# Second block of a transformer kernel: window attention's projections by token tiles, two ScalarE steps in the recurrence's operands

## The chip, the cores and the metric

The program runs on one core of a Trainium2 chip as one launch. The metric is the device time of that core in microseconds (us). Three runs of the kernel before took 4450.48, 4458.26 and 4474.45 us; their median is 4458.26 us.

## The reference

A two-part network over 1024 tokens of 1024 features: a first block (two mixers, each followed by a mixture of experts, in float32), and a second block, which the change touches. Of the second block only its start matters here. It normalises the tokens x and 256 context tokens, multiplies both with one projection `w_in`, and cuts the columns of the result into queries, keys and values of a window attention, the inputs of a recurrence, and gates:

```python
h  = modulate(rmsnorm_2(x, norm1_g), shift1, scale1)
hc = modulate(rmsnorm_2(xc, norm1_g), modc[0], modc[1])
q, k, v, rw, gl = jnp.split(h @ w_in, IN_SPLITS, axis=-1)       # 512, 128, 128, 1696, 2048 columns
qc, kc, vc, rwc, glc = jnp.split(hc @ w_in, IN_SPLITS, axis=-1)
q = apply_rope(q.reshape(B, L, N_Q_HEADS, HEAD_DIM), cos, sin)
k = apply_rope(k.reshape(B, L, N_KV_HEADS, HEAD_DIM), cos, sin)
ya = latent_window_attention(q, k, v, kc, vc, sink)
r_l, v_l, hg_l, kk_l, dirs_l = rwkv_prepare(short_conv(rw, conv_w), decay_w0, decay_w2,
                                            iclr_a0, iclr_a2, k_k, k_a)
# in rwkv_prepare, for two directions d, with k the recurrence's keys:
#   w_log = -softplus(-(decay_w0[d] + tanh(hw) @ decay_w2[d])) - 0.5
#   a = sigmoid(iclr_a0[d] + ha @ iclr_a2[d]);  k_d = k * (1 + (a - 1) * k_a)
```

## The kernel before

Every float32 operand of a product is split into two float32r parts, a high one (`hi`, a ScalarE copy, L111) and the rest (`lo`, a VectorE subtraction, L116), and a product is three matmuls (high by high, low by high, high by low). The eight PSUM banks are shared out by use: here A 3, S 2, T 2 (transposes) and M 1.

The start of the second block is `block2` (L1163). Its stages follow each other in this order.

1. Norms, `block2_norms` (L1229): eight token tiles of 128 x 1024 in pairs. For a pair, squares on ScalarE (L1261) and a weighted sum of them on VectorE (L1262) give the factors; VectorE scales (`ht`, L1272), GpSimd adds the shift (L1273). `to_hT` transposes a tile on TensorE (L185, eight transposes of 128 x 128 into two banks of T) and splits it into `hH` and `hL`, features by tokens. Two context tiles go the same way into `cH` and `cL`.
2. Low ranks and gate of the recurrence, in `Rwkv.project` (L1531): `conv(W, 0, 64, 12, ..)` and `conv(W, 64, 96, 13, ..)` (L1582, L1583). A `conv` is a product of up to 128 features with all tokens, in token pieces of 512, 512 and 256, that is 24 matmuls of each, and a convolution of three taps. Their weights, 160 columns, are loaded before the norms' tokens.
3. The operand stage: four times (`ft`) two `conv` of 128 features (keys `uk`, receptances `ur`), `norms` (L1670, whose first matmuls are L1684), and `operands` (L1697), which goes through three token pieces and two directions. There a tanh on ScalarE (L1717) is followed by `l + 1` on VectorE (L1718), prefix sums (L1721), exponentials and products on VectorE, and on GpSimd `kd = ta * kh0 + kh1` (L1741) with two products (L1742, L1743). A matmul into bank M (L1754) takes `kd` at the end of a piece.
4. Four `conv` of the recurrence's values, and what is left of the window.

The window's projection is the generator `Window.project` (L1369). Its first piece makes keys and values of ten token tiles: 24 matmuls of 128 x 256, a ScalarE copy `qo` (L1398), the rotation of the keys on VectorE (`rotate`, L832 to L837), transposes, `qkH`, `qkL`, and stores to `wv_d` and `wk_d`. The second and third pieces make the two halves of the queries (L1407), eight tiles of 128 x 256 each. `more` hands them out: the first behind `operands` of ft 0, the second behind ft 1, the third at the end (L1591, L1200). The instructions of the engines are put in order by a scheduler that follows this program order by dependencies and buffers, so that window work is spread over the stage that follows.

Of the kernel before, what the change touches and what calls it, by code (L numbers as in the profile page):

```python
# [34 lines left out]
D = 1024  # L35
# [8 lines left out]
class K:  # L44
    """Engines, pools and the few operations that every phase uses."""
# [62 lines left out]
    # float32 as the sum of two float32r parts, exact  # L108
# [9 lines left out]
    def row_max(s, pool, todo, mx):  # L118
        """Largest of scores + mask by rows, one column of mx each."""
# [5 lines left out]
    def to_rows(s, pool, cols, n, *dst):  # L125
        """The negatives of columns, one after the other in rows of partition 64."""
# [13 lines left out]
    def weights(s, raw, ring, src, shape, leng=None, queue=None):  # L140
        """A block of weights, loaded and split."""
# [11 lines left out]
    def rstd(s, ss, n, scale, eps, name):  # L153
        """(ss * scale + eps) ** -0.5, few elements per partition."""
# [6 lines left out]
    def bcast(s, pool, ap, n, name, parts=128, **kw):  # L161
        """A row of n values in DRAM on every partition."""
# [5 lines left out]
    def norm_pair(s, pool, xs, gb, outs, eps=EPS, gb2=None):  # L168
        """Two token tiles normalised over their 1024 features and scaled by gb (plus gb2)."""
# [11 lines left out]
    def transpose4(s, src, n=4):  # L181
        """Four [128, 128] blocks of a token tile, transposed into one PSUM bank."""
# [5 lines left out]
    def to_hT(s, src, hH, hL, t):  # L188
        """A token tile [128, 1024] into features by tokens, split."""
# [12 lines left out]
# ---------------------------------------------------------------- even mixer  # L202
# [4 lines left out]
def even_mixer(k, es_out, x_d, w, mod_d):  # L207
    """x_d: DRAM [1024, 1024]. w: DRAM inputs. Returns the output projection and what it takes. The second
    block's modulation goes by the way."""
# [42 lines left out]
def proj_tile(k, hH, hL, W, t, n):  # L252
    """h of token tile t times a block of weights given in chunks of two k-tiles."""
# [74 lines left out]
def even_project(k, es, w, raw, ring, hH, hL, q_d, k_d, v_d):  # L328
    """Queries, keys and values, rotated, in their two parts: q_d, k_d [part, head, feature, token], v_d [part, head,
    token, feature]."""  # L330
# [36 lines left out]
NQ = 4  # heads whose operands are on chip at a time  # L367
# [31 lines left out]
def even_head(k, p2, mb, mc, me, h, slot, q_d, k_d, v_d, a_d, r_d):  # L399
# [13 lines left out]
    # values, by tokens shifted by half a tile and by residue classes of 4  # L413
# [12 lines left out]
    with k.tc.high_priority(offset=HP):  # L426
        # row maxima of both key sets
# [28 lines left out]
    def attend():  # L456
# [21 lines left out]
        # band of 64 tokens to either side  # L478
# [3 lines left out]
        def pv(b, c, v, P):  # L482
            # one accumulation group per bank: what is not yet written is overwritten
# [25 lines left out]
        # dilations 4 and 16, within the residue classes of 4  # L509
# [16 lines left out]
def normalise(k, p2, O, r_row, dst, shape=None, more=None):  # L526
    """Rows 0..63 of O over its row 64 into DRAM. more adds to the row, spread over the partitions."""
# [12 lines left out]
class OutProj:  # L540
    """x + a @ w_out by token tiles; a: features by tokens in DRAM, one tile of 128 features each."""
# [40 lines left out]
# ---------------------------------------------------------------- mixture of experts  # L582
# [5 lines left out]
class Moe:  # L588
    """Expert choice over the tokens of x1; x_d gathers x1 and what the experts add to it."""

    def __init__(s, k, es, i, w, x_d):
# [8 lines left out]
        # the router takes the tokens before their norm: its weights by the norm's  # L600
# [38 lines left out]
    def rank(s, x, last):  # L639
        """The best of every expert so far and these: in order, but for the last time."""  # L640
# [9 lines left out]
        if s.best is not None:  # L650
            # the best of two lists: the one against the other from its end; then sorted
# [14 lines left out]
    def choose(s):  # L666
        """Which slot of which expert a token takes: those above the last of the best by their order, then the
        first of its equals."""
        k, p = s.k, s.p1
        # token number and gate in parts that bfloat16 carries exactly  # L670
# [19 lines left out]
        # how many up to a token, and how many above in all  # L690
# [16 lines left out]
    def gather(s, p, e):  # L707
        """The tokens of an expert, their numbers and gates."""
# [18 lines left out]
    def experts(s):  # L727
        k, w, i = s.k, s.w, s.i
        s.es.close()
        with ExitStack() as es:  # L730
# [11 lines left out]
            # in the order of use: the first products of an expert go ahead of the last of the expert before  # L742
# [65 lines left out]
# ---------------------------------------------------------------- odd mixer  # L808
# [31 lines left out]
def odd_mixer(k, es_out, x_d, w):  # L840
    """x_d: DRAM [1024, 1024]. w: DRAM inputs. Returns the output projection and what it takes."""
    a_d = [k.dram.tile([128, T], F32, name=f"a_do{i}") for i in range(8)]
    r_d = k.dram.tile([16, T], F32, name="r_d1")
    # operands of the attentions in their two parts, features by tokens, by heads or pairs of heads
# [25 lines left out]
def odd_proj(k, es, x_d, w, d):  # L870
# [23 lines left out]
    # ranks: queries, keys and values, rotary keys  # L894
# [27 lines left out]
    def heads(x, n, g, r, t):  # L922
        """Norms and rotations of n heads of a token tile."""
# [8 lines left out]
    def split_rows(src, dst, half, m):  # L932
        """Four token tiles' columns src(t) as features by tokens, split, into dst[part]."""
# [50 lines left out]
    # from the ranks to the heads  # L984
# [39 lines left out]
def odd_attention(k, es, d, a_d, r_d):  # L1024
# [13 lines left out]
    def head(n, h):  # L1038
# [25 lines left out]
        # row maxima of the scores, negated, into a row of the queries' operand  # L1064
# [41 lines left out]
# ---------------------------------------------------------------- second block  # L1106

TC = 256  # context tokens
C = 64  # tokens of a chunk of the recurrence
# [53 lines left out]
def block2(k, x_d, w, mod_d, out):  # L1163
# [7 lines left out]
    with ExitStack() as es:  # L1171
# [28 lines left out]
        for _ in more:  # L1200
            pass
# [1267 lines left out]
```

## Time and profile before

| | |
|---|---|
| runs, median | 4458.26 us (4450.48 to 4474.45) |
| the profiled execution, span | 4467.4 us |
| TensorE busy, mean granted clock | 3963.4 us (89%), 0.928 of full speed |
| VectorE, ScalarE, GpSimd busy | 66%, 41%, 25% |
| the stages of the change | 2248 to 2722 us of the span |

The trace gives one execution, and every time in the sections below is counted from the start of its span. A granted clock of 1.00 is TensorE's level of 2.4 GHz, one of 0.50 its level of 1.2 GHz; values between them are a mixture over the stretch. In a timeline a matmul's duration is its time from first to last of a pipeline, so the distance of two starts tells the cost of one.

### The profile page before, as it was taken

To read this page: it belongs to the slowest core of one execution; us is meant where nothing else is said; L and a number is where in the kernel's file an instruction comes from. 1 tells how busy PE (TensorE), PEld (TensorE's weight loads), DVE (VectorE), ACT (ScalarE), POOL (GpSimd) and SP (SyncE) were. 2 spreads that over 40 slices of the span, in tenths; PEclk is the share of its full clock that TensorE was granted. 3 is DMA by queue.
4 is the path that set the end of the run, shared out by engine and by line. 5 is a ranking of instruction groups with operands and counts; after the bars stand their busy time and mean duration, and the time that the engine had idled before them with its cause. 6 is when DMAs were issued, how large, how long until landed. Compare 5 with 4: busy or idle time off the path is not lost. (4 is left out here: it accounts for less than half of the span.)

```text
span 4467.4 us, 65652 instructions
## 1 busy us (share of the span) xinstructions
PE 3963.4 (89%) x24208; PEld 3233.3 (72%) x24208; DVE 2938.6 (66%) x5925; ACT 1815.5 (41%) x3066; POOL 1109.1 (25%) x1069
## 2 busy tenths in 40 slices
PE   7898995897978999689948997999988899999998
PEld 7797884775855666567737776777777678888887
DVE  8656658896678875879866793766677565332334
ACT  3223332675447775257634452333333432212212
POOL 2211212121213433112133363222244511101101
PEclk9998997999989999889968998989998999999999
DMA  5758435898267543569933446555756662111112
GB/s 163 228 170 187 110 112 186 304 367 279 82 189 176 116 102 93 188 238 365 329 111 118 148 148 181 138 142 137 166 145 147 190 210 88 57 48 48 49 55 85
DMA packets 568286, 714.12 MB, mean 160 GB/s; under 512 B 243636, under 2 KB 355332, under 8 KB 567964
## 3 DMA queue, kind: packets, MB, share of 16 engines
q1 hardware_dynamic: 467788, 510.50, 37.3%
q0 software_dynamic: 42480, 144.62, 11.9%
q10 hardware_dynamic: 57696, 54.80, 3.8%
q8 instruction: 191, 3.13, 0.3%
q14 instruction: 131, 1.07, 0.1%
HBM read 555.84 MB, written 153.53 MB: 159 GB/s over the span
## 5 line engine op out<-in xcount | busy, mean ns | idle before, releaser
L116 DVE TENSOR_TENSOR w_l<-w_raw,w_h 128x2048 fp32r<-128x2048 f32 (+5 forms) x336 | 592.2, 1769 | 194.1 <-ACT w_h L111 192.9
L111 ACT ACTIVATE w_h<-w_raw 128x2048 fp32r<-128x2048 f32 (+4 forms) x344 | 507.2, 1487 | 437.4 <-PE psO L138 254.5
L138 PE MATMUL psA<-w_h,hH 128*128 128x256 f32 (+3 forms) x896 | 292.6, 330 | 28.9 <-ACT w_h L111 13.7
L138 PE MATMUL psA<-w_l,hH 128*128 128x256 f32 (+3 forms) x896 | 292.6, 327 | 1.9 <-DVE w_l L116 1.7
L138 PE MATMUL psA<-w_h,hL 128*128 128x256 f32 (+3 forms) x896 | 291.3, 326 | 0.0
L116 POOL TENSOR_TENSOR uL<-relu,uH 128x512 fp32r<-128x512 f32 x64 | 82.6, 1291 | 571.9 <-ACT uH L111 571.9
L138 PE MATMUL psA<-w_h,xH 128*128 128x512 f32 x512 | 208.5, 409 | 11.6 <-ACT xH L111 8.8
L138 PE MATMUL psA<-w_l,xH 128*128 128x512 f32 x512 | 211.1, 412 | 7.1 <-DVE w_l L116 6.9
L138 PE MATMUL psA<-w_h,xL 128*128 128x512 f32 x512 | 206.1, 404 | 4.3 <-DVE xL L116 4.3
L138 PEld LDWEIGHTS psA<-w_h,hH 128*128 128x128 f32 x896 | 174.5, 196 | 41.6 <-ACT w_h L111 15.1
L2287 DVE TENSOR_TENSOR relu<-relu 128x512 f32<-128x512 f32 x64 | 44.3, 693 | 238.2 <-ACT relu L2286 238.2
L116 DVE TENSOR_TENSOR PL<-P,PH 128x512 fp32r<-128x512 f32 x192 | 171.1, 903 | 27.3 <-ACT PH L111 27.1
L138 PEld LDWEIGHTS psA<-w_l,hH 128*128 128x128 f32 x896 | 175.3, 196 | 10.4 <-DVE w_l L116 4.6
L138 PE MATMUL psA<-ghH,gwH 128*128 128x256 f32 x512 | 169.6, 331 | 14.5 <-DMA ghH<-hs_d 5.0
L138 PEld LDWEIGHTS psA<-w_h,hL 128*128 128x128 f32 x896 | 175.1, 195 | 5.3 <-issue 2.6
L805 POOL DMA_INDIRECT x_d<-yo,idx x32 | 69.8, 2182 | 421.5 <-ACT yo L804 417.5
L111 ACT ACTIVATE gwH<-gw 128x256 fp32r<-128x256 f32 x256 | 103.3, 414 | 163.1 <-PE psA L138 121.0
L138 PE MATMUL psA<-ghH,gwL 128*128 128x256 f32 x512 | 161.2, 315 | 1.3 <-POOL gwL L116 1.0
L138 PE MATMUL psA<-ghL,gwH 128*128 128x256 f32 x512 | 160.4, 313 | 0.0
L116 POOL TENSOR_TENSOR gwL<-gw,gwH 128x256 fp32r<-128x256 f32 x128 | 97.5, 765 | 248.3 <-ACT gwH L111 207.5
L111 ACT ACTIVATE PH<-P 128x512 fp32r<-128x512 f32 x256 | 154.5, 629 | 6.5 <-POOL PL L116 1.3
L116 POOL TENSOR_TENSOR PL<-P,PH 128x512 fp32r<-128x512 f32 x64 | 90.9, 1420 | 231.2 <-ACT PH L111 178.2
(654 smaller groups left out, 11896.8 us busy)
## 6 DMA issues: line engine op xcount, KB each, us to landing
w_raw<-in_moe_w_gate_dram SPq DMA_DIRECT2D x64, 1024.0 KB
w_raw<-in_moe_w_up_dram SPq DMA_DIRECT2D x64, 1024.0 KB
w_raw<-in_moe_w_down_dram SPq DMA_DIRECT2D x64, 1024.0 KB
gw<-in_w_in_t_dram POOLq DMA_DIRECT2D x64, 512.0 KB, 5.5
wada<-in_w_ada_dram POOLq DMA_DIRECT2D x48, 512.0 KB, 5.8
w_raw<-in_w_mlp_up_dram SPq DMA_DIRECT2D x16, 1024.0 KB
w_raw<-in_w_mlp_down_dram SPq DMA_DIRECT2D x16, 1024.0 KB
AR<-ar_d SPq DMA_DIRECT2D x40, 256.0 KB
```

Source lines behind the costliest of these rows:

```text
L111: s.a.activation(h, x, AF.Copy)
L116: (eng or s.v).tensor_tensor(l, x, f(h), op=ALU.subtract)
L138: s.t.matmul(ps, a, b, start=first and i == 0, stop=last and i == n - 1)
L805: k.g.indirect_dma_start(out=s.x_d[:, :], out_offset=off, in_=y, in_offset=None, compute_op=ALU.add)
L2287: k.v.tensor_tensor(a, a, a, op=ALU.mult)
```

## The change

The window's keys, values and first half of the queries are made inside the norms: right behind the transposes of token tile t, `done(t)` multiplies it by 512 columns of weights at once (keys, values, first half of the queries), copies, rotates, transposes, splits and stores. The four weight blocks of 128 x 2 x 512 (2 MB) and the tables `cosW`, `sinW` are loaded ahead of the norms' tokens. The pools of the later weights are opened behind the norms, in the same space. The second half of the queries (`A.rest`) comes behind `R.project`, as before. In `operands` the steps `l + 1` and `kd` go to ScalarE.

```diff
@@ block2
-        raw = k.pool(es, "b_raw", 2)
-        ring = k.pool(es, "b_ring", 5)
+        A.open_project(es)
+        with ExitStack() as es1:
+            block = blocks(k.pool(es1, "b_raw1", 4), k.pool(es1, "b_ring1", 4))
+            tile_ = A.first(block, hH, hL, cH, cL)
+            block2_norms(k, w, x_d, mod_d, hH, hL, cH, cL, rs, tile_)
+        block = blocks(k.pool(es, "b_raw", 2), k.pool(es, "b_ring", 5))
         p0 = k.pool(es, "rp0", 1)
-        block2_norms(k, w, x_d, mod_d, hH, hL, cH, cL, rs)
         R.ranks_weights(p0)
...
-        more = A.project(es, block, hH, hL, cH, cL)
-        R.project(block, hH, hL, cH, cL, more, stores())
-        for _ in more:
-            pass
+        R.project(block, hH, hL, cH, cL, stores())
+        A.rest(block, hH, hL)
@@ block2_norms
                 k.to_hT(h, hH, hL, t)
+                done(t)
-        ca = k.bcast(p1, mod_d[7], D, "ca")
-        cs = k.bcast(p1, mod_d[6], D, "cs")
+        ca = k.bcast(p1, mod_d[7], D, "ca", tag="g2")
+        cs = k.bcast(p1, mod_d[6], D, "cs", tag="gf")
...
             k.to_hT(xs[t], cH, cL, t)
+            done(8 + t)
@@ Window
+    def first(s, block, hH, hL, cH, cL):
+        k = s.k
+        W = block((512, 0))
+
+        def tile_(t):
+            ps = proj_tile(k, hH, hL, W, t, 512) if t < 8 else proj_tile(k, cH, cL, W, t - 8, 256)
+            o = s.pp.tile([128, 256], F32, name="qo")
+            k.a.activation(o, ps[:, 0:256], AF.Copy)
+            k.a.dma_start(s.v_d[128 * t:128 * t + 128], o[:, 128:256])
+            s.store(o[:, 0:128], 2, s.k_d, t, t < 8)
+            if t < 8:
+                o = s.pp.tile([128, 256], F32, name="qo")
+                k.a.activation(o, ps[:, 256:512], AF.Copy)
+                s.store(o, 4, s.q_d[:, 0:4], t, True)
+
+        return tile_
@@ Rwkv.project
-                for _ in range((1, 1, 0, 0)[ft]):
-                    next(more)
@@ Rwkv.operands
-                k.v.tensor_scalar(l, l, 1.0, None, op0=ALU.add)
+                k.a.activation(l, l, AF.Copy, bias=1.0)
...
-                k.g.tensor_scalar(kd, ta, s.kh[:, ft, 0:1], s.kh[:, ft, 1:2], op0=ALU.mult, op1=ALU.add)
+                k.a.activation(kd, ta, AF.Identity, scale=s.kh[:, ft, 0:1], bias=s.kh[:, ft, 1:2])
```

How this moves the instructions is seen in their order on two engines. First TensorE before, at the start of the norms: `psO` is the last product of the experts, `ht` a normalised token tile, `hH` and `hL` its transposed parts, and the products 64 wide are those of the low ranks.

```order
L138 MATMUL psO<-w_h,yL 128x512
L185 MATMUL psT<-c_ident,ht 128x128 x28
L138 MATMUL psA<-hH,w_h 64x512
L185 MATMUL psT<-c_ident,ht 128x128 x8
L138 MATMUL psA<-hL,w_h 64x512
L138 MATMUL psA<-hH,w_l 64x512
```

Three and a half tiles are transposed in one go, and the products between later ones are single products of the low ranks. TensorE after, from the last matmul of one token tile's product to the first of the next's (`qo` holds keys or queries; in brackets the semaphores that a row waits for):

```order
L138 MATMUL psA<-w_h,hL 128x512
L185 MATMUL psT<-c_ident,qo 128x128 [waits DVE_49,Activation_49]
L185 MATMUL psT<-c_ident,qo 128x128 [waits DVE_49,PE_49,Activation_49]
L185 MATMUL psT<-c_ident,qo 128x128
L185 MATMUL psT<-c_ident,ht 128x128 [waits DVE_49,Pool_49]
L185 MATMUL psT<-c_ident,ht 128x128 x3
L185 MATMUL psT<-c_ident,ht 128x128 [waits DVE_49]
L185 MATMUL psT<-c_ident,ht 128x128 x3
L138 MATMUL psA<-w_h,hH 128x512 [waits Activation_49]
```

The transposes of the next token tile now stand behind those of this tile's keys and queries, and all 24 matmuls of a tile stand together. The products of low ranks and gate follow the last context tile. VectorE before, in the norms' first tiles:

```order
L116 TENSOR_TENSOR w_l<-w_raw,w_h 128x512
L116 TENSOR_TENSOR hL<-psT,hH 128x4x128
L156 TENSOR_SCALAR m_n_20792<-ss_20778 128x2
L116 TENSOR_TENSOR hL<-psT,hH 128x4x128
L1264 COPY rs<-r_n_20840 128x2
L1266 TENSOR_TENSOR ss_20831<-ss_20831,r_n_20840 128x2
L1262 ISA sq,ss_20884<-sq,g_20703 128x1024
```

VectorE after, between the same two products (`rot_2` are the keys' products in the rotation, `rot_4` the queries'):

```order
L833 TENSOR_TENSOR rot_4_32_20845<-qo,sinW 128x128
L834 TENSOR_TENSOR rot_4_32_20846<-qo,sinW 128x128
L835 TENSOR_TENSOR rot_4_32_20847<-qo,cosW 128x128
L836 TENSOR_TENSOR qo<-rot_2_32_20824,rot_2_32_20825 128x2x32
L837 TENSOR_TENSOR qo<-rot_2_32_20826,rot_2_32_20827 128x2x32
L836 TENSOR_TENSOR qo<-rot_4_32_20844,rot_4_32_20845 128x4x32
L837 TENSOR_TENSOR qo<-rot_4_32_20846,rot_4_32_20847 128x4x32
L116 TENSOR_TENSOR qkL<-psT,qkH 128x128
L116 TENSOR_TENSOR qkL<-psT,qkH 128x256
L116 TENSOR_TENSOR hL<-psT,hH 128x4x128
```

The sums of both rotations stand behind the queries' products, and `hL` of the next tile behind both `qkL`; the statistics of all tiles (`ss`, `m_n`) have moved ahead of the first rotation. VectorE before, in the operand stage:

```order
L1738 TENSOR_TENSOR ar<-r,F 128x8x64
L1745 TENSOR_TENSOR bf<-ta,E 128x8x64
L1718 TENSOR_SCALAR l<-l 128x256
L116 TENSOR_TENSOR qkL<-psT,qkH 128x256
L832 TENSOR_TENSOR rot_4_32_22920<-qo,cosW 128x128
L833 TENSOR_TENSOR rot_4_32_22921<-qo,sinW 128x128
L834 TENSOR_TENSOR rot_4_32_22922<-qo,sinW 128x128
L835 TENSOR_TENSOR rot_4_32_22923<-qo,cosW 128x128
L116 TENSOR_TENSOR qkL<-psT,qkH 128x256
L1721 SCALAR_TENSOR_TENSOR F<-reset,l 128x256
L1751 TENSOR_TENSOR kd<-kd,r 128x512
L1744 SCALAR_TENSOR_TENSOR ta<-ta,nk 128x512
```

and after, at the same step:

```order
L1750 TENSOR_TENSOR ar<-r,F 128x8x64
L1756 SCALAR_TENSOR_TENSOR ta<-ta,nk 128x512
L1749 SCALAR_TENSOR_TENSOR ar<-nk,F 128x8x64
L1757 TENSOR_TENSOR bf<-ta,E 128x8x64
L1733 SCALAR_TENSOR_TENSOR F<-reset,l 128x256
L1763 TENSOR_TENSOR kd<-kd,r 128x512
L1756 SCALAR_TENSOR_TENSOR ta<-ta,nk 128x512
L1738 TENSOR_TENSOR F<-tot,F 128x256
```

The rotations, `qkL` and `l + 1` are gone from this place. On SyncE's queue, `cosW`, `sinW` and eight loads of 128 x 2 x 256 now stand ahead of the first token load, where four of 128 x 2 x 160 stood.

## Rows read from the trace of the kernel before

**Rows 1.** busy times by stretch, from the norms to the window's last piece.

```profile
core 0: us, PE busy (x) PEld busy (x) DVE busy (x) ACT busy (x) POOL busy (x), PEclk, DMA share, GB/s
2248.20:2278.80 30.60, 0.04 (x2) 0.02 (x1) 14.24 (x24) 10.48 (x19) 7.93 (x6) 0.56 0.86 273
2278.80:2334.90 56.10, 30.31 (x125) 20.69 (x125) 43.90 (x64) 17.59 (x31) 27.27 (x23) 0.65 0.14 45
2334.90:2354.70 19.80, 19.80 (x101) 15.85 (x102) 12.14 (x17) 11.11 (x15) 0.00 (x0) 0.86 0.11 32
...
2396.60:2477.30 80.70, 72.01 (x459) 64.20 (x459) 62.15 (x131) 37.18 (x88) 35.91 (x23) 0.96 0.43 142
2477.30:2554.60 77.30, 67.04 (x415) 59.66 (x414) 64.91 (x129) 36.46 (x84) 37.95 (x23) 0.93 0.45 151
2554.60:2615.40 60.80, 54.60 (x286) 47.28 (x284) 53.81 (x72) 31.68 (x66) 33.41 (x23) 0.92 0.48 172
2615.40:2670.00 54.60, 49.93 (x257) 43.01 (x257) 49.12 (x63) 29.31 (x66) 33.29 (x23) 0.91 0.35 121
2670.00:2722.50 52.50, 37.95 (x275) 35.96 (x275) 22.92 (x74) 14.05 (x33) 14.08 (x21) 0.90 0.75 202
```

**Rows 2.** timeline of the first token tile of the norms: start, duration, engine, instruction, idle.

```profile
2278.78 1.97 PE L185 MATMUL psT<-c_ident,ht 128*128 128x128 f32 x8 [30.56 <-POOL ht L1273]
...
2279.93 0.60 ACT L111 ACTIVATE hH<-psT 128x512 fp32r<-128x512 f32 x1 [4.51 <-PE psT L185]
...
2285.05 0.68 DVE L116 TENSOR_TENSOR hL<-psT,hH 128x512 fp32r<-128x512 f32 x1
...
2286.46 1.21 DVE L1262 CUSTOM_DVE_ANT_0 sq<-sq,g 128x1024 f32<-128x1024 f32 x1
```

**Rows 3.** timeline of the last query tile, all engines.

```profile
2719.34 0.38 ACT L1407 ACTIVATE qo<-psA 128x256 f32<-128x256 f32 x1
...
2719.82 0.28 DVE L832 TENSOR_TENSOR rot<-qo,cosW 128x128 f32<-128x128 f32 x1
...
2720.82 0.28 DVE L837 TENSOR_TENSOR qo<-rot,rot 128x128 f32<-128x128 f32 x1
...
2721.26 0.41 PE L185 MATMUL psT<-c_ident,qo 128*128 128x128 f32 x2 [2.23 <-DVE qo L837]
...
2722.12 0.42 DVE L116 TENSOR_TENSOR qkL<-psT,qkH 128x256 fp32r<-128x256 f32 x1 [1.01 <-ACT qkH L111]
```

**Rows 4.** timeline of TensorE in the last products of low ranks and gate.

```profile
2334.86 1.11 PE L185 MATMUL psT<-c_ident,xt 128*128 128x128 f32 x4 [5.79 <-DVE cL L116]
...
2339.08 0.63 PE L138 MATMUL psA<-hL,w_h 128*96 128x512 f32 x1
2339.51 0.63 PE L138 MATMUL psA<-hH,w_l 128*96 128x512 f32 x1
...
2340.36 0.40 PE L138 MATMUL psA<-hL,w_h 128*96 128x512 f32 x1
2340.59 0.39 PE L138 MATMUL psA<-hH,w_l 128*96 128x512 f32 x1
```

**Rows 5.** busy times and clock of two short stretches in the norms, columns as above.

```profile
2313.00:2316.00 3.00, 1.07 (x9) 0.79 (x7) 1.83 (x2) 1.08 (x2) 1.84 (x2) 1.00 0.00 0
2316.00:2319.00 3.00, 2.00 (x9) 1.66 (x10) 1.62 (x4) 1.20 (x2) 2.88 (x10) 0.57 0.12 23
```

**Rows 6.** groups of VectorE, operand stage: line, shapes, count, busy us, mean ns, idle.

```profile
L1718 DVE TENSOR_SCALAR l<-l 128x512 f32<-128x512 f32 x14 | 6.4, 456 | 0.1
...
L1718 DVE TENSOR_SCALAR l<-l 128x256 f32<-128x256 f32 x8 | 5.5, 692 | 0.0
```

**Rows 7.** the same view of GpSimd.

```profile
L1741 POOL TENSOR_SCALAR kd<-ta,kh 128x512 f32<-128x512 f32 x16 | 28.4, 1772 | 18.1 <-PE psM L1754 9.3 <-ACT w_h L111 4.7 <-PE psT L185 3.1
...
L1741 POOL TENSOR_SCALAR kd<-ta,kh 128x256 f32<-128x256 f32 x8 | 9.8, 1226 | 0.8
```

**Rows 8.** the same view of ScalarE.

```profile
L1733 ACT ACTIVATE E<-F 128x512 f32<-128x512 f32 x8 | 5.0, 627 | 2.8 <-PE psT L1684 2.8
```

More of the change, by code (lines that the diff above doesn't have):

```diff
@@ L1179, in block2, with blocks, block @@
         cL = hp.tile([128, 8, TC], F32R, name="cL")
+        A.open_project(es)
+        def blocks(raw, ring):
+            def block(lo, n=256, queue=None):
+                los = (lo,) if isinstance(lo, int) else lo
+                return [k.weights(raw, ring, [w["w_in_t"][:, 2 * j:2 * j + 2, x:x + n] for x in los],
+                                  [128, 2, n * len(los)], queue=queue) for j in range(4)]
+            return block
+        with ExitStack() as es1:
[3 more added lines that the diff above has]
+        block = blocks(k.pool(es, "b_raw", 2), k.pool(es, "b_ring", 5))
         p0 = k.pool(es, "rp0", 1)
-        block2_norms(k, w, x_d, mod_d, hH, hL, cH, cL, rs)
         R.ranks_weights(p0)
-        def block(lo, n=256, queue=None):
-            los = (lo,) if isinstance(lo, int) else lo
-            return [k.weights(raw, ring, [w["w_in_t"][:, 2 * j:2 * j + 2, x:x + n] for x in los],
-                              [128, 2, n * len(los)], queue=queue) for j in range(4)]
         def stores():
@@ L1226, in block2, with block2_norms @@
         merge(k, es, w, ya_d, yr_d, gl_d, x_d, rs, mod_d, out)
-def block2_norms(k, w, x_d, mod_d, hH, hL, cH, cL, rs):
+def block2_norms(k, w, x_d, mod_d, hH, hL, cH, cL, rs, done):
     with ExitStack() as es:
@@ L1233, in block2_norms @@
         p = k.pool(es, "bn2", 2)
-        gf = k.bcast(p1, w["final_norm"], D, "gf", eng=k.a)
-        g2 = p1.tile([128, D], F32, name="g2")
+        gf = k.bcast(p1, w["final_norm"], D, "gf", eng=k.a, tag="gf")
+        g2 = p1.tile([128, D], F32, name="g2", tag="g2")
         k.a.activation(g2, gf, AF.Square)
@@ L1367, in __init__, with open_project @@
         s.r_d = k.dram.tile([16, 512], F32, name="wr_d")
[L1369 removed]
+    def open_project(s, es):
         k = s.k
         p1 = k.pool(es, "wp1", 1)
[L1373 to L1411 removed]
@@ new lines, in open_project, with store @@
+        s.pp = k.pool(es, "wp2", 2)
+        s.cosW, s.sinW = (p1.tile([128, 8, 32], F32, name=n) for n in ("cosW", "sinW"))
+        k.d.dma_start(s.cosW, k.cst["cosW"])
+        k.d.dma_start(s.sinW, k.cst["sinW"])
+    def store(s, x, n, dst, t, rope):
+        k, p2, cosW, sinW = s.k, s.pp, s.cosW, s.sinW
+        if rope:
+            x3 = x.rearrange("p (h c) -> p h c", h=n)
+            cs, sn = (y[:, t, None].to_broadcast([128, n, 32]) for y in (cosW, sinW))
+            rotate(k, p2, x3[:, :, 0:32], x3[:, :, 32:64], cs, sn, [128, n, 32], k.v)
+        ps = k.transpose4(x, n // 2)[:, :64 * n]
+        H, L = (p2.tile([128, 256], F32R, name="qk" + a)[:, :64 * n] for a in "HL")
+        k.hi(H, ps)
+        k.lo(L, ps, H)
+        for j, o in enumerate((H, L)):
+            k.a.dma_start(f(dst[j, :, :, 128 * t:128 * t + 128].rearrange("(r h) c t -> (h c) r t", h=2)),
+                          f(o.rearrange("p (r t) -> p r t", t=128)))
@@ L1413, in open, with rest @@
+    def rest(s, block, hH, hL):
+        k = s.k
+        W = block(256)
+        for t in range(8):
+            ps = proj_tile(k, hH, hL, W, t, 256)
+            o = s.pp.tile([128, 256], F32, name="qo")
+            k.a.activation(o, ps, AF.Copy)
+            s.store(o, 4, s.q_d[:, 4:8], t, True)
     def open(s, es):
@@ L1529, in __init__, with project @@
         s.bon_d = k.dram.tile([128, 8, 8], F32, name="u_bon")
-    def project(s, block, hH, hL, cH, cL, more, stores):
+    def project(s, block, hH, hL, cH, cL, stores):
         k, w = s.k, s.w
```

35 lines of the change are left out of this document (removed).

## Prediction

> **What bounds the kernel now.** I read the busy time by stretch first, then the timelines of the norms and of one query tile, then the operand stage's groups of instructions with what their engines waited for.
>
> The stretches show three regimes [rows 1]. Between the experts' last product and the first token transposes TensorE has 30.60 us and works 0.04; the transfers are 0.86 busy there, so this part waits for data. In the next 56.10 us VectorE works 43.90 and TensorE 30.31 at a granted clock of 0.65: the norms on VectorE set the pace, and TensorE has room, though at a poor clock. Low ranks and gate fill the 19.80 us up to 2354.70. The operand stage, 2396.60 to 2670.00, is full: in its first two quarters, which carry window work, TensorE works 72.01 of 80.70 and 67.04 of 77.30 us and VectorE 62.15 and 64.91; in the last, which carries none, 49.93 and 49.12 of 54.60. So window work is dear where it stands today, and the norms have unused TensorE time. What matters is whether that time can be used by work that depends on the norms tile by tile.
>
> **Part one: what the operand stage gives back.** The two quarters with window work are 80.7 and 77.3 us long, the one with a little of it left over 60.8, the free one 54.6 [rows 1]. Four free quarters would be 4 x 54.6 = 218.4 instead of 273.4 us: 55.0 us saved. The second half of the queries stays in the last stretch (52.50 us) and is costed at no change; its cover is the recurrence's loads, which wait for the operands, and if they came first a query tile would cost at most its 3 us of rows [rows 3].
>
> **Part two: the ScalarE steps.** `l + 1` takes VectorE 6.4 + 5.5 = 11.9 us of the stage [rows 6], 3.0 a quarter. `kd` takes GpSimd 28.4 + 9.8 = 38.2 us [rows 7], 9.5 a quarter. On ScalarE a step of 128 x 512 takes 0.627 us (an exponential of that shape [rows 8]); I take it for both, and about two thirds of that for the 256-wide ones: 16 x 0.63 + 8 x 0.42 = 13.4 us for each step, 6.7 a quarter for both. ScalarE has 29.31 of 54.60 us busy there and goes to about 36: the idle quarter-time hides it. VectorE goes from 49.1 to 46.1, so a quarter can't be under about 47 us while VectorE sets it; with nothing gained it stays 54.6. I take 52, nearer the upper end because TensorE's 49.93 does not shrink. Four quarters of 52 are 208: with part one 65 us saved (55 to 85).
>
> **Part three: what the norms pay.** The first tile's product needs both parts of its tile. `hL` of tile 0 ends at 2285.05 + 0.68 = 2285.7 today [rows 2]. VectorE's order now has two more sums of squares ahead of its second half, 1.21 us each by the next of them [rows 2]: start at 2288. The extra 1.6 MB of weights ahead of the token loads I cost at nothing, since those loads wait for the experts' scatter anyway; at 273 GB/s [rows 1] it would be 6 us if that cover is gone.
>
> One tile then is a closed loop: product, copy, rotation, transposes, split, the next tile's transposes and split, product. In a 256-wide query tile the copy starts at 2719.34, the first rotation step at 2719.82, the last at 2720.82, the transposes at 2721.26, and `qkL` ends at 2722.12 + 0.42 = 2722.54: 3.2 us [rows 3]. The keys' copy and their six smaller steps add about 0.38 + 0.7 in front, but their `qkL` ends before the queries' does. The next tile's first four transposes wait only for the keys' bank, so they go beside the queries' split; then come 0.60 for `hH` and 0.68 for `hL` [rows 2]. Together about 5.4 us from the last matmul of a tile to the first of the next (4.5 to 6.5). Nothing else stands in TensorE's queue in that time: the next tile's transposes are behind this tile's, and the low ranks' products behind all tiles.
>
> The 24 matmuls of 512 columns cost 0.43 us each at the lower clock (2339.08 to 2339.51) and 0.23 at the higher (2340.36 to 2340.59) [rows 4]: 10.3 or 5.5 us. In these rows TensorE works on without a gap from 2334.86 and the higher level comes by 2340.36, 5.5 us later. In the norms a stretch of 3 us with 1.07 us of work is still at 1.00, and the next is at 0.57 [rows 5]. So a 5.4 us gap with some 2.5 us of transposes in it costs the level, I expect, and a tile gets it back in its second half: ten or eleven matmuls at 0.43 and the rest at 0.23 make 7.6 us. A tile takes 5.4 + 7.6 = 13.0 us (10.9 all fast, 15.7 all slow).
>
> So the first product ends at 2288 + 7.6 = 2295.6, the eighth at 2295.6 + 7 x 13.0 = 2386.6. The context's two products have 24 matmuls of half the width, 2.8 to 5.2 us, taken as 4.1; ahead of the first stands a whole gap of 5.4, ahead of the second one without queries and rotation, about 3.4: 9.5 and 7.5 us more, 2403.6. Then the 144 matmuls of low ranks and gate, 96 of 512 columns and 48 of 256, which today partly fill the gaps of the norms: 96 x 0.23 + 48 x 0.115 = 27.6 us, 2.5 for a slow start and 2 for weights that now are split only there, in all 32: 2435.6. Today the same point is 2354.7 [rows 1]. The norms pay 81 us (56 with everything at the higher level and no waits; 113 with everything at the lower and 6 us of late loads).
>
> **The sum.** 81 - 65 = 16 us longer, against the profiled execution's span of 4467.4 us, which is 9 above the median of the runs and inside their spread. Against the median that is 4458 + 16 = 4474 us. About 0.5% (22 us: 4436 and 4480.5) can be told from no change, so the forecast is no measurable change, close to the slow border.
>
> **Rivals.** (A) The products never reach the higher level: each tile starts slow and its gap ends the climb before it pays. For it: the whole norm stage has 0.65 [rows 1], and [rows 5] shows a level lost in a 3 us stretch. Against it: the climb in [rows 4] took 5.5 us, less than a slow product of 10.3. A tile then takes 15.7 us, the eighth product ends at 2288 + 10.3 + 110 = 2408, the stage at about 2460: it pays 105, and the sum is 105 - 65 = +40, 4498 us. It decides once the gap plus the climb is longer than the product. The Trainium skill, "TensorE: Matmul & The Clock Gate", section "HAM oscillation — how this bites in real kernels", describes this pattern, short bursts of matmuls with waits between that each begin at the low clock; it would side with A, while the rows give each tile a fast second half.
>
> (B) The loop stays short and fast and the operand stage falls to VectorE's own time: a tile of 10.9 us, the stage pays 56, quarters of 47 us save 85, the sum is -29: 4429 us. For it: transposes fill part of each gap, and in the free quarter VectorE is 90% busy, so that what leaves it counts. VectorE's steps of one shape scatter there: `l + 1` of 256 columns has a mean of 692 ns, longer than the 456 ns of 512 columns [rows 6], which speaks for interference that may go when GpSimd does less. The Trainium skill, "Perfetto Trace Analysis", section "Optimizing Scalar/DVE Operations", says that GpSimd and VectorE share a port to SBUF; by that B's quarters gain from the moved `kd` too. Against it: TensorE's 49.93 us in the same quarter.
>
> (C) ScalarE becomes the queue that waits. `kd` on GpSimd waited 9.3 us for the matmul that frees its buffer (`psM`, L1754), 4.7 and 3.1 us for others [rows 7]. On ScalarE that wait holds up the tanh and the copies behind it, from which TensorE's banks come free. If half of these 17 us and the queueing of 6.7 us a quarter land on the path, a quarter is 57 us and only 46 are saved: +35, 4493 us.
>
> **Chances.** The forecast (clock regained within each tile, quarters of 52) 0.40, A 0.25, B 0.20, C 0.15. The forecast's own range is 4452 to 4496. B gives nearly all of the chance of faster by over 0.5%, 0.18. A and C lie mostly above 4480.5, and so does a third of the forecast: slower 0.40. Within 0.5%: 0.42. The range for 8 in 10 takes in C, most of A with late loads, and most of B: 4432 to 4512.
>
> **What would show it.** Right: in the changed profile TensorE between the first and the eighth 512-wide product shows blocks of 24 at a distance of about 13 us with a granted clock that rises inside each; low ranks and gate end near 2436; the quarters of the operand stage are alike, 50 to 54 us; `kd` on ScalarE takes about 0.63 us. A shows blocks at 0.43 us throughout, B blocks 11 us apart or quarters under 49 us, C waits of ScalarE's `kd` with quarters of 56 us or more. The forecast is wrong in its base if the transposes of the next tile, its split and its product do not follow the keys' and queries' transposes one after the other, or if the token loads come late.

## The result

The changed kernel takes 4506.33 us (median of 4 runs, 4504.99 to 4507.78) against 4462.57 us of the kernel before (4 runs, 4450.48 to 4474.45, with one more run of it). The ratio is 1.0099, 95% interval 1.0078 to 1.0119: 44 us slower, clear of the 0.5% that can be told. The prediction had 4474 us with a range of 4432 to 4512 us, 0.42 for no measurable change and 0.40 for slower. The time is inside the range, but above the forecast's own 4452 to 4496 us, and the outcome that it held likeliest, no measurable change, did not come.

The two profiled executions are 4467.4 and 4503.0 us long, 35.6 apart. The profiled span of the kernel before is 4.8 us above its median and that of the changed kernel 3.3 us below, which makes the medians' 44. The table cuts both at the same events, by the starts of matmuls. The "first gate product" is the first with `g2H`, just behind the low ranks' and gate's products with `w_in`. The first row is ahead of everything that the change touches: there the two executions differ by 5 us.

| from / to | before | after | difference |
|---|---|---|---|
| start / last matmul of the experts | 2247.8 | 2253.1 | +5.2 |
| ... / first transposes of the norms | 31.0 | 33.3 | +2.3 |
| ... / first gate product (norms, window tiles, low ranks) | 82.5 | 168.6 | +86.1 |
| ... / first norms' matmul of the operand stage | 35.3 | 35.4 | +0.1 |
| ... / last matmul into bank M (four quarters) | 273.3 | 235.1 | -38.2 |
| ... / first product of the recurrence | 81.0 | 67.8 | -13.2 |
| ... / end | 1716.5 | 1709.8 | -6.7 |

The busy times by stretch of the changed kernel, as in [rows 1] (stretch, its length, busy time of TensorE, its weight loads, VectorE, ScalarE and GpSimd, granted clock, share of the DMA engines, GB/s):

```profile
2253.30:2286.40 33.10, 0.17 (x1) 0.00 (x0) 17.07 (x24) 12.31 (x18) 8.43 (x6) 0.55 0.81 261
2286.40:2413.20 126.80, 92.99 (x345) 70.18 (x345) 59.63 (x171) 27.83 (x63) 23.60 (x13) 0.75 0.18 53
2413.20:2449.00 35.80, 30.69 (x147) 21.32 (x147) 17.57 (x28) 15.04 (x24) 2.57 (x10) 0.90 0.23 64
...
2490.30:2550.30 60.00, 56.70 (x298) 48.55 (x296) 50.50 (x65) 36.90 (x76) 27.54 (x17) 0.94 0.49 171
2550.30:2610.20 59.90, 56.04 (x292) 47.85 (x291) 52.33 (x70) 39.54 (x86) 25.90 (x17) 0.94 0.43 163
2610.20:2670.00 59.80, 39.79 (x198) 32.35 (x197) 49.73 (x68) 36.28 (x79) 24.78 (x17) 0.80 0.39 141
2670.00:2725.50 55.50, 43.35 (x226) 38.17 (x226) 43.86 (x57) 32.13 (x71) 25.68 (x17) 0.82 0.27 99
2725.50:2766.50 41.00, 27.56 (x223) 26.04 (x221) 19.29 (x66) 10.84 (x26) 16.23 (x27) 0.94 0.89 249
```

The norms' stretch is now 126.80 us, with 345 TensorE rows where [rows 1] has 125 in 56.10; TensorE works 92.99 us of it at a clock of 0.75. The four quarters are 60.0, 59.9, 59.8 and 55.5 us. In the last two TensorE works 39.79 and 43.35 us at 0.80 and 0.82, VectorE 49.73 and 43.86. TensorE has less to do there than in the same quarters before, its clock is lower, and the quarters are no shorter (60.8 and 54.6 us before).

The loop between two tiles' products, in the changed kernel's timeline (start, duration, engine, line, instruction, in brackets the idle time before it and what ended it):

```profile
2341.78 0.39 PE L138 MATMUL psA<-w_h,hL 128*128 128x512 f32 x1
2342.20 0.38 ACT L1407 ACTIVATE qo<-psA 128x256 f32<-128x256 f32 x1 [6.65 <-PE psA L138]
...
2342.62 0.23 DVE L832 TENSOR_TENSOR rot<-qo,cosW 128x64 f32<-128x64 f32 x1 [5.76 <-ACT qo L1407]
...
2344.45 0.28 DVE L837 TENSOR_TENSOR qo<-rot,rot 128x128 f32<-128x128 f32 x1
2344.47 0.81 PE L185 MATMUL psT<-c_ident,qo 128*128 128x128 f32 x3 [2.31 <-DVE qo L837]
...
2345.55 1.08 PE L185 MATMUL psT<-c_ident,ht 128*128 128x128 f32 x4 [0.27 <-DVE qkL L116]
2346.04 0.38 ACT L111 ACTIVATE qkH<-psT 128x256 fp32r<-128x256 f32 x1 [0.95 <-DVE qkL L116]
2346.46 0.42 DVE L116 TENSOR_TENSOR qkL<-psT,qkH 128x256 fp32r<-128x256 f32 x1 [1.05 <-ACT qkH L111]
2346.68 0.60 ACT L111 ACTIVATE hH<-psT 128x512 fp32r<-128x512 f32 x1 [0.25 <-PE psT L185]
...
2347.31 0.69 DVE L116 TENSOR_TENSOR hL<-psT,hH 128x512 fp32r<-128x512 f32 x1 [0.43 <-ACT hH L111]
...
2347.33 0.79 PE L138 MATMUL psA<-w_h,hH 128*128 128x512 f32 x1 [0.69 <-ACT hH L111]
```

From the last matmul of one tile (2341.78) to the first of the next (2347.33) there are 5.5 us; ScalarE's copy, twelve rotation steps, transposes, split, the next tile's transposes and its split follow each other, and TensorE's transposes in between are short. 5.4 us were predicted from [rows 2, 3]. This is the shortest of the seven gaps. They are 5.5 to 6.6 us but for one of 9.4 behind the second product, where VectorE first scales both context tiles (L176, 2.48 us from 2314.27) and starts the rotation at 2316.67; the mean is 6.4. Inside the product that follows, the clock comes back:

```profile
2351.33 0.63 PE L138 MATMUL psA<-w_l,hH 128*128 128x512 f32 x1
...
2351.76 0.60 PE L138 MATMUL psA<-w_h,hL 128*128 128x512 f32 x1
...
2352.18 0.40 PE L138 MATMUL psA<-w_h,hH 128*128 128x512 f32 x1
...
2352.43 0.39 PE L138 MATMUL psA<-w_l,hH 128*128 128x512 f32 x1
```

Two starts are 0.43 us apart up to 2352.18 and 0.25 or less from there: 4.9 us after the product's start. In the second to eighth product this takes 1 to 4.9 us, and from the first to the last start of its 24 matmuls such a product takes 7.4 us in the mean. The eight products end at 2300.2, 2312.7, 2328.9, 2342.0, 2355.6, 2369.3, 2383.2 and 2396.7 us, 13.8 us apart in the mean (13.0 predicted, 15.7 by rival A). Without the 5 us that the execution was late before the change, and the 2 us of token loads, the first and the eighth would be at 2293 and 2389; 2295.6 and 2386.6 were predicted.

The two moved steps on ScalarE, in the operand stage (count, busy us, mean ns, idle time before them), and the largest wait of that engine there:

```profile
L1753 ACT ACTIVATE kd<-ta,kh 128x512 f32<-128x512 f32 x16 | 12.9, 803 | 1.0 <-PE psM L1766 1.0
...
L1730 ACT ACTIVATE l<-l 128x512 f32<-128x512 f32 x14 | 8.7, 622 | 0.1
...
L1753 ACT ACTIVATE kd<-ta,kh 128x256 f32<-128x256 f32 x8 | 4.8, 597 | 0.6 <-POOL bf L1755 0.6
...
L1730 ACT ACTIVATE l<-l 128x256 f32<-128x256 f32 x8 | 3.3, 412 | 0.1
```

```profile
ACT ta L1729 <- DVE bf L1757: 27.5, 15, 4.9
```

`kd` takes 803 and 597 ns, `l + 1` 622 and 412; 630 and 420 were taken for both. ScalarE's one wait for bank M (1.0 us) is far from the 9.3 us that GpSimd had [rows 7], so rival C's mechanism did not come, although its sign of quarters of 56 us or more did in three of the four; ScalarE's wait for VectorE's `bf` was there before (27.6 us).

### The profile page after: what moved, and what is told of

Same layout as the page of the kernel before. It is cut to its first block, busy times and chain, and to the rows that moved or that the text cites. A ratio compares the mean times of both kernels' runs of the same rounds, so it can differ in the third digit from the quotient of the medians.

```text
span 4503.0 us, 65307 instructions
## 1 busy us (share of the span) xinstructions
PE 3980.3 (88%) x24016; PEld 3235.1 (72%) x24016; DVE 2918.2 (65%) x5897; ACT 1841.7 (41%) x3110; POOL 1070.6 (24%) x1045
## 5 line engine op out<-in xcount | busy, mean ns | idle before, releaser
L116 DVE TENSOR_TENSOR w_l<-w_raw,w_h 128x2048 fp32r<-128x2048 f32 (+4 forms) x332 | 589.9, 1784 | 193.7 <-ACT w_h L111 192.3
L138 PE MATMUL psA<-w_h,hH 128*128 128x384 f32 (+3 forms) x832 | 287.2, 348 | 26.2 <-ACT w_h L111 13.6
L138 PE MATMUL psA<-w_l,hH 128*128 128x384 f32 (+3 forms) x832 | 284.3, 342 | 1.9 <-DVE w_l L116 1.7
L138 PE MATMUL psA<-w_h,hL 128*128 128x384 f32 (+3 forms) x832 | 283.3, 341 | 2.5 <-DVE hL L116 2.5
L138 PEld LDWEIGHTS psA<-w_h,hH 128*128 128x128 f32 x832 | 163.7, 198 | 43.8 <-ACT w_h L111 14.9
L138 PEld LDWEIGHTS psA<-w_l,hH 128*128 128x128 f32 x832 | 164.2, 197 | 13.4 <-DVE w_l L116 4.6
L138 PEld LDWEIGHTS psA<-w_h,hL 128*128 128x128 f32 x832 | 163.6, 197 | 11.8 <-DVE hL L116 3.2
```

The source lines that it names most:

```text
L116: (eng or s.v).tensor_tensor(l, x, f(h), op=ALU.subtract)
L138: s.t.matmul(ps, a, b, start=first and i == 0, stop=last and i == n - 1)
```

## The experiments

Medians are from several runs of each kernel beside runs of the kernel before on the same chip; medians of different chips differ by some us, so ratios are compared. Theory 1: the closed loop of a tile is what the norms pay, and a quarter of the operand stage is about 60 us without window work, whoever does the two steps. Its rivals are named in the expectations. Theory 3 came up with the first four runs.

**The ScalarE steps alone, and the window's part alone.** The first run is the kernel before with the change's edit of `Rwkv.operands` and nothing else.

> The kernel before with the two ScalarE steps alone. Theory 1 (a quarter of the operand stage without window work is 60 us whoever does these steps, so they are worth next to nothing): 0 to 8 us faster than before, 4455 to 4463 us. Theory 2 (a quarter would be 52 to 55 us, but the steps on ScalarE hold up its queue): 12 to 20 us slower than before, 4475 to 4483 us.

Measured: 4510.16 us against 4474.53, ratio 1.0076 (1.0059 to 1.0093), 36 us slower. Neither theory has the total. The operand stage is 266.8 us, 6.5 shorter than before (quarters of 81.4, 76.1, 58.5 and 50.8), and the tail up to the recurrence as before. The loss stands behind all that: from the recurrence's first product to the end the profile has 1768.2 us instead of 1716.5, in code that this edit does not touch.

The opposite edit, the changed kernel with both steps back on VectorE and GpSimd:

> The changed kernel with the two steps back on VectorE and GpSimd. Theory 1: within 8 us of the changed kernel, 4503 to 4514 us, quarters of 60 to 62 us. Theory 2: 15 to 25 us faster than the changed kernel, 4482 to 4491 us, quarters of 54 to 55 us.

Measured: 4562.76 us, ratio 1.0193 (1.0176 to 1.0211): 88 us slower than before, a total that misses both theories. The stage ahead of the recurrence agrees with theory 1: quarters of 62.3, 58.7, 60.3 and 60.1 us, 241.3 in all, 6.2 more than in the changed kernel. So the two steps are worth 6 us in the operand stage, with or without window work in it, about half of the 11.9 us that VectorE gives away [rows 6]. But the time from the recurrence to the end is 1756.0 us, 46 more than in the changed kernel. The two parts of the change don't add up: alone they cost 36 and 88 us, together 44. What differs is again the recurrence.

**The quarter without window work.**

```diff
-                for _ in range((1, 1, 0, 0)[ft]):
+                for _ in range((0, 0, 0, 0)[ft]):
                     next(more)
```

> The kernel before with all three pieces of the window's projection behind the last convolutions: norms as before, operand stage without window work. Theory 1: quarters of 60, 60, 60 and 55 us, 235 us from the first norms' matmul of the first quarter to the last matmul into bank M, 38 less than before; the last stretch grows by the two pieces' 50 us of TensorE and some stalls, so 10 to 30 us slower than before, 4472 to 4492 us. What the prediction assumed: four quarters of 54.6 us, 218 us, 55 less than before, and 4455 to 4470 us.

Measured: 4498.46 us, ratio 1.0053 (1.0033 to 1.0072), 24 us slower, a total as theory 1 has it. But 20 us of it lie behind the recurrence's first product (1736.3 us to the end instead of 1716.5); up to there the profile is 8 us longer than before. The four quarters by stretch:

```profile
2399.00:2461.30 62.30, 56.46 (x297) 48.83 (x295) 54.07 (x72) 32.31 (x68) 36.25 (x23) 0.95 0.46 159
2461.30:2520.00 58.70, 54.05 (x277) 46.64 (x277) 51.78 (x71) 31.21 (x69) 33.44 (x23) 0.91 0.45 168
2520.00:2580.70 60.70, 42.61 (x211) 35.28 (x210) 53.95 (x76) 30.94 (x68) 33.71 (x23) 0.78 0.40 143
2580.70:2640.80 60.10, 44.39 (x226) 38.55 (x227) 49.20 (x64) 28.64 (x64) 33.02 (x23) 0.79 0.31 110
```

They are 62.3, 58.7, 60.7 and 60.1 us with no window work at all, 241.8 in all. That settles the mis-sized term: taking the window's keys, values and first queries out of the operand stage is worth 273.3 - 241.8 = 31.5 us, not 55. The 54.6 us of the last quarter in [rows 1] were no measure of a free quarter, for two reasons. VectorE has less to do there than in the three others: 49.12 us, where here it works 54.07, 51.78 and 53.95 in the first three. And the last quarter itself, with the same 49.20 us of VectorE, is 60.1 us long here. Nearly all of the 5.5 us are one wait of VectorE for the transposes of `kd` (L1693), in the kernel before and then in this run. Below each stands the stretch of TensorE's matmuls ahead of these transposes:

```profile
2624.70 0.69 DVE L1694 SCALAR_TENSOR_TENSOR nk<-nk,psT 128x512 f32<-128x512 f32 x1 [1.95 <-PE psT L1693]
...
2618.30:2624.10 5.80, 5.80 (x27) 4.74 (x28) 4.07 (x6) 3.15 (x8) 1.64 (x1) 1.00 0.00 0
```

```profile
2592.91 0.69 DVE L1694 SCALAR_TENSOR_TENSOR nk<-nk,psT 128x512 f32<-128x512 f32 x1 [7.28 <-PE psT L1693]
...
2583.00:2592.20 9.20, 9.20 (x30) 7.16 (x30) 2.63 (x5) 2.42 (x7) 1.81 (x1) 0.69 0.00 1
```

The transposes stand behind matmuls of the next `conv`. These run at a clock of 1.00 in the kernel before and at 0.69 here, behind a gap of 2.9 us on TensorE. The changed kernel's last quarter has the same wait (6.87 us, with 0.68 ahead of it). So what makes the last quarter longer here is mostly TensorE at a lower clock, by the two traces; no run held the clock fixed. In the first three quarters VectorE's own time is 87 to 89% of the length.

**The loop opened.** The product of tile t - 1 now stands behind the transposes of tile t, and the transposes of its keys and queries, with their split and stores (`finish`), in the middle of the next product:

```diff
+            k.mm(ps, pairs[:12], True, False)
+            if t > 0:
+                finish(t - 1)
+            k.mm(ps, pairs[12:], False, True)
...
         def tile_(t):
...
+            if t > 0:
+                product(t - 1)
```

> The changed kernel with the closed loop opened: the product of a token tile stands behind the transposes of the next tile, and the transposes of its keys and queries stand in the middle of the next product. Theory 1 (the loop of copy, rotation, split and next split is what the norms pay): a tile takes 7.5 to 9 us in place of 13.8, the norms, low ranks and gate end 40 to 50 us earlier, 4456 to 4468 us. Rival (the lower clock is what they pay, and it stays low in the norms): a tile takes 11 to 12.5 us, 4485 to 4496 us.

Measured: 4492.99 us, ratio 1.0036 (1.0015 to 1.0056), 18 us slower than before and so some 28 us faster than the changed kernel. In the profile the second and the eighth product end at 2299.5 and 2356.3 us, 9.5 us a tile (7.5 to 9 expected), and the first gate product comes 165.1 us after the experts instead of 201.9: 37 us earlier (40 to 50 expected), with the same matmuls. The clock from 2300 to 2360 us is 0.91 to 1.00. So the loop, with the lower clock that its gaps bring, is worth 37 of the 88 us that the norms pay; this run does not part the two. The other 51 are about what the ten products cost at the higher level with nothing waiting, by the starts of [rows 4] an estimated 8 x 5.5 + 2 x 2.8 = 50 us. The whole is behind the expectation because from the recurrence's first product to the end it takes 1749.0 us instead of 1709.8. In its trace, first a place where the transposes stand inside a product at the higher clock, then one where VectorE is held up:

```profile
2317.46 0.39 PE L138 MATMUL psA<-w_l,hH 128*128 128x512 f32 x1
...
2317.69 0.38 PE L185 MATMUL psT<-c_ident,qo 128*128 128x128 f32 x2
...
2317.83 0.48 PE L138 MATMUL psA<-w_h,hL 128*128 128x512 f32 x1
...
2322.76 2.43 POOL L1278 TENSOR_TENSOR ht<-ht,gs 128x1024 f32<-128x1024 f32 x1 [6.47 <-DVE ht L1277]
2322.87 2.40 DVE L834 TENSOR_TENSOR rot<-qo,sinW 128x64 f32<-128x64 f32 x1
```

A rotation step of 128 x 64 takes 2.40 us here, where its neighbours of that shape take 0.22, and it ends with GpSimd's addition of 2.43 us that started 0.11 us before it.

**Why the recurrence differs.** The instructions of a stage are put in order by a scheduler that goes through the whole program, so an edit in one stage moves the order in all that follow: TensorE's order from the recurrence on differs between the kernel before and the one with the ScalarE steps alone in 4190 of 9006 rows, and by the two traces more than a third of the changed kernel's rows there stand elsewhere. Theory 3: this order alone is worth tens of us. A barrier of all engines ahead of the recurrence makes the scheduler begin there from the same state:

```diff
+        k.tc.strict_bb_all_engine_barrier()
         more = others(k, w, A, h_d, gl_d)
```

> The kernel before with a barrier of all engines ahead of the recurrence, so that the scheduler puts the recurrence in order from the same start whatever came before. It is the base for the next three; its own time only shows what the barrier and another order cost. Theory 3 (the recurrence's length is set by the order that the scheduler happens to give it): recurrence and gates take anything from 800 to 865 us, total 4455 to 4540 us.

> The same barrier in the kernel with the two ScalarE steps alone; TensorE's order from the recurrence on differs from the kernel with the barrier in 36 of 9098 rows (without barriers 4190 of 9006). Theory 3: recurrence and gates as long as with the barrier alone, within 4 us, and the whole 4 to 10 us shorter by the operand stage. Rival (the two steps themselves leave something that slows the recurrence): 35 to 55 us longer than with the barrier alone.

Measured: 4496.84 us (4481.84 to 4507.98) for the kernel before with the barrier, ratio 1.0052 (1.0032 to 1.0072); 4503.78 us (4489.23 to 4511.02) with the ScalarE steps as well, 1.0073 (1.0049 to 1.0096). The intervals overlap: where the order is the same but for 36 rows, the 36 us of the ScalarE steps are down to 7, which can't be told from none. So the two steps do not slow the recurrence by what they do. The barrier costs the kernel before 25 us (4471.33 without it) and leaves the one with the ScalarE steps where it was against that kernel (1.0076 and 1.0073), as if the kernel before had lost a good order. But a barrier also lets the engines run empty, so this pair alone does not part the order from other things that a stage hands on. The recurrence and gates of the two profiles, without and then with the ScalarE steps:

```profile
2751.80:3596.80 845.00, 748.20 (x8372) 598.49 (x8372) 554.31 (x1573) 306.20 (x751) 286.14 (x366) 0.88 0.59 145
```

```profile
2752.90:3578.70 825.80, 730.43 (x8373) 585.90 (x8373) 552.37 (x1573) 306.03 (x751) 285.30 (x366) 0.90 0.61 149
```

These two stretches have the same instructions in nearly the same order, and still differ by 19 us, so one profile of the recurrence is good to some 20 us only; the profiled executions lie 11 us above the first median and 14 below the second. The medians carry the verdict. The operand stages are 271.7 and 266.6 us.

> The same barrier in the changed kernel. Theory 3: 30 to 45 us longer than the kernel before with the barrier, nearly all of it ahead of the barrier (the norms pay 88, the operand stage gives back 38 and the last stretch 13); recurrence and gates within 15 us. Rival (work moved early makes the recurrence itself shorter): recurrence and gates 20 us or more shorter.

> The same barrier in the kernel with the loop opened by one tile. Theory 1: 35 to 45 us shorter than the changed kernel with the barrier, so within 10 us of the kernel before with the barrier.

Measured: 4554.36 us for the changed kernel with the barrier, 1.0205 (1.017 to 1.0241), 58 us over the kernel before with the barrier, more than expected; 4529.37 us for the opened loop, 1.013 (1.0107 to 1.0153). From the experts' end to the recurrence's first product the profiles have 503.6 (before), 548.8 (changed) and 514.7 us (loop opened): 45 and 11 us more. Opening the loop is worth 25 us here by the medians, less than expected, and 34 us ahead of the recurrence. The barrier did not make these orders equal (by the traces about one in seven and one in four of TensorE's rows there still stand elsewhere), so their recurrences (840.0 and 858.8 us) can't be compared with confidence.

The test without any edit ahead of the recurrence:

```diff
-SHARES = (30, 30, 25, 25, 20, 10, 10, 10, 5, 5)
+SHARES = (28, 30, 25, 25, 20, 12, 10, 10, 5, 5)
```

> The kernel before with SHARES, the number of window and gate pieces handed out behind the recurrence's first ten groups, 28 and 12 in its first and sixth place instead of 30 and 10. Everything up to the recurrence keeps its order; from there 1822 of 9006 rows of TensorE differ. Theory 3 (the order that the recurrence happens to get is worth tens of us, and the kernel before has a good one): 10 to 45 us slower than before, norms and operand stage as before within 3 us. Rival (orders are worth little, and what slowed the other kernels comes from the stages ahead): within 8 us of before.

Measured: 4494.94 us against 4466.17, ratio 1.006 (1.0041 to 1.008), 29 us slower, as theory 3 has it. The stages up to the recurrence are as before (499.2 us from the experts' end against 503.1). Recurrence and gates by stretch, of the kernel before, the changed kernel, the ScalarE steps alone and the other shares, in this order:

```profile
2750.90:3557.40 806.50, 722.78 (x8285) 581.22 (x8285) 550.62 (x1546) 298.44 (x736) 278.34 (x357) 0.90 0.61 149
```

```profile
2793.20:3598.20 805.00, 726.79 (x8293) 586.51 (x8293) 546.92 (x1547) 299.96 (x737) 278.13 (x358) 0.89 0.60 150
```

```profile
2748.30:3610.10 861.80, 743.81 (x8291) 597.77 (x8291) 547.52 (x1549) 301.39 (x740) 277.53 (x359) 0.86 0.57 141
```

```profile
2735.80:3571.80 836.00, 738.93 (x8283) 598.11 (x8283) 540.08 (x1546) 300.16 (x736) 277.53 (x357) 0.87 0.58 145
```

They are 806.5, 805.0, 861.8 and 836.0 us, with the same number of matmuls to within 10. TensorE stands still for 84, 78, 118 and 97 us of them and works longer at a lower clock (0.90 and 0.89 against 0.86 and 0.87). The kernel before and the changed one have the two shortest of all thirteen profiles; nine others have 826 to 862 us, and the two of the last pair below 809 and 814. As one profile is good to 20 us, the medians are the better witness: less what each profile gains or loses between the experts' end and the recurrence, they leave for the rest some 7 us more than before in the changed kernel, 41 in each of its two parts alone, 16 in the quarter without window work, 25 in the opened loop and 33 with the other shares. That the changed kernel cost little more than its stages, and its two parts so much alone, therefore lies behind the stages. That an order can do this is shown by the other shares; that it did so in the two parts is argued from that run and the barrier.

**A last pair.** The opened loop, with the norms' shift on VectorE, and the same with the other shares:

```diff
-                k.g.tensor_tensor(h, h, gs, op=ALU.add)
+                k.v.tensor_tensor(h, h, gs, op=ALU.add)
```

> The kernel with the loop opened by one tile, and the norms' shift (ht + gs) on VectorE instead of GpSimd. In that kernel's trace a rotation step of 0.28 us on VectorE took 2.40 us while GpSimd's addition of 2.43 us ran. If the one holds up the other, a tile takes 8 to 8.5 us instead of 9.2, and norms, low ranks and gate end 6 to 10 us earlier; if not, VectorE's 1.2 us more a tile makes it 0 to 8 us later. The total hangs on the order that the recurrence gets: 4450 to 4510 us.

> The same with the changed SHARES of the run before. Norms and operand stage as there within 2 us. Theory 3: the recurrence differs by 10 us or more from the run before, one way or the other; 4440 to 4510 us.

Measured: 4463.44 us against 4466.17, ratio 0.9992 (0.9977 to 1.0007), and 4462.32 us, 0.9997 (0.9978 to 1.0015). Both take as long as the kernel before and some 45 us less than the changed one. The first gate product comes 157.9 us after the experts, 7 us earlier than with GpSimd's addition (8.8 us a tile). The same rotation step in that trace:

```profile
2346.78 0.22 DVE L833 TENSOR_TENSOR rot<-qo,sinW 128x64 f32<-128x64 f32 x1
2346.91 0.22 DVE L834 TENSOR_TENSOR rot<-qo,sinW 128x64 f32<-128x64 f32 x1
2347.05 0.22 DVE L835 TENSOR_TENSOR rot<-qo,cosW 128x64 f32<-128x64 f32 x1
```

It takes 0.22 us, as its neighbours (the expectation's 0.28 us is the time of the steps of 128 x 128). The recurrence and gates are 809.0 and 814.4 us: the shares that cost the kernel before 29 us cost this one nothing that can be told, against theory 3's 10 us or more here. So what an edit of the order is worth hangs on the order that it meets. No kernel tried beats the kernel before by more than can be told.

## Where the prediction held, and where it failed

- "The norms pay 81 us": measured 88.4 (2.3 to the first transposes and 86.1 up to the first gate product). The closed loop was there; its gaps were 6.4 us in the mean instead of 5.4 (the terms listed for 5.4 add up to 5.6), its products 7.4 instead of 7.6, a tile 13.8 instead of 13.0. The clock was lost in each gap and came back inside each product. Low ranks and gate took 36 us instead of 32, since TensorE waits 4.6 us between their two products for ScalarE's copies, which stand behind the low ranks' weights. This step held, and the fourth run shows what the loop is worth: with it opened the same work takes 37 us less.
- Rival A, blocks at the lower clock throughout, did not come: 13.8 us a tile is not 15.7, and at most 4.9 us into a product the higher level is back. The Trainium skill, "TensorE: Matmul & The Clock Gate", section "HAM oscillation — how this bites in real kernels", describes bursts that each start at the low clock after a wait. The trace agrees in that all eight products begin at the lower clock (starts 0.43 us apart); the second half of each does not stay there (0.23).
- "Four quarters of 52 are 208: 65 us saved" is the step that failed. Measured are 235.1 us and 38.2 saved. The size of a quarter without window work was read from the last one (54.6 us), but without window work quarters are 59 to 62 us (third run): the last one holds less VectorE work than the others, and TensorE ran at 0.91 in it, where the last quarter of the third run has 0.79. Of the 38.2 us about 32 are the window's work and 6 the ScalarE steps (first and second run).
- "The ScalarE steps": hidden as costed (ScalarE 32.13 to 39.54 us a quarter), worth 6 us in the stage instead of 10; "nearer the upper end because TensorE's 49.93 does not shrink" was the wrong reason. TensorE's busy time did shrink, to 39.79, and the quarter did not.
- The last stretch was costed at no change; it is 13.2 us shorter, and 6 in the pair with the barrier. No run was made on it, but the two traces show 310 TensorE rows there instead of 369 (44.68 us busy instead of 56.54): the last rows of the values' `conv` and some products of the queries now run inside the operand stage.
- Not seen at all: an early edit puts the whole recurrence in a new order, and from there on the runs differ by up to 50 us. In this pair it was worth -6.7 us by the profiles and about +7 by the medians, luck that the forecast had no part in; in a run of either part alone it would have been off by 40.

With 88 for 81 and 38 for 65 the sum is +50; the shorter last stretch and recurrence take off 20, and the 5 us by which the execution was late put back some. That is the 35.6 us of the profiles. The two stages that the prediction worked out miss by 34 us together, in the same direction. That the time is still inside the range owes something to luck: without the 13 us of the last stretch, costed at nothing, it would be some 4519 us, above 4512.

## What to carry to other kernels

Work that fills an engine's idle time in a stage is only cheap if it does not join the chain that sets the stage's pace; put one tile of distance between a product and what needs its result. Take the length of a stage "without" some work from a run that leaves the work out, not from its last repetition: the repetitions need not hold the same work, nor keep their clock when the work goes. Where a scheduler orders the program, compare the stages of two traces at the same events before believing a total: an edit's own gain can be smaller than what the new order does to a stage that it never touches.

## What the runs showed of the hardware

- A VectorE step of 128 x 64 that normally takes 0.22 us took 2.40 us beside a GpSimd addition of 128 x 1024 (2.43 us) and ended with it (opened loop); with that addition on VectorE (1.22 us) it took 0.22 us, and the stage was 7 us shorter though VectorE had more to do. The Trainium skill, "Perfetto Trace Analysis", section "Optimizing Scalar/DVE Operations", says that the two engines share a read port to SBUF; the trace agrees in that the step waited. VectorE's `hL`, which reads one input from PSUM, took its usual 0.68 us beside such an addition (2334.55 in the same trace).
- ScalarE's step with a scale and a bias per partition takes 803 ns for 128 x 512, where one with constants takes 622 ns.
- With less work on TensorE in a quarter of nearly the same length (39.79 us instead of 54.60), its granted clock fell from 0.92 [rows 1] to 0.80. In the last quarter VectorE then waited 6.87 us for transposes behind matmuls at 0.68, where it had waited 1.95 us behind matmuls at 1.00.
